# The last 256 tokens normalised as rows, a first layer with another order of transfers, splits and products, and low parts of fills on GpSimd: one change to a two-layer encoder step

## The chip, the cores and the metric

The kernel runs on one core of a Trainium2 chip. Its engines work side by side and meet at semaphores: the tensor engine (PE, with its weight loads PEld), VectorE (DVE), ScalarE (ACT), GpSimd (POOL), and SyncE (SP), which here issues all the transfers. The metric is the device time of one execution, in microseconds (us); lower is better.

## The reference

One step of a two-layer streaming encoder on 512 prompt tokens and 64 sample tokens (576 in all, `d_model` 1024). Everything is float32.

```
layer 0:  mixed = [ mLSTM(x), retention(x) ] from one input projection x @ w_in
          (4 heads each; per-head norm, gates; chunk by chunk), then mixed @ w_out
          x = LayerNorm(ALPHA * x + mixed @ w_out)
          x = LayerNorm(ALPHA * x + (silu(x @ w_g) * (x @ w_u)) @ w_down)
layer 1:  latent attention over past 256 rows and the new rows, with a chunk mask
          x = LayerNorm(ALPHA * x + attention(x) @ w_out)
          x = LayerNorm(ALPHA * x + (silu(x @ w_g) * (x @ w_u)) @ w_down)
```

The outputs are x of both groups and the states and cache rows that the layers leave.

## The kernel before

**Products in three parts.** Each float32 product is made of three products of a faster type: a value is split into a high part (ACT copies it into the type fp32r, L364 for weights, L600 for x) and a low part (the value less the high part, by a subtraction on DVE, L362 and L601). `fm` and `tm` issue high x high, low x high and high x low for each 128 rows of the contraction. `fm` gives a result with features on the partitions and tokens along the free dimension (weights stationary); `tm` gives rows, tokens on the partitions and 512 columns of features along it (activations stationary). `tms` is `tm` for the 64 sample tokens, with the high and low part of x side by side in the tile XS.

**Where activations lie.** Z holds x with features on the partitions, 8 blocks of 576 tokens. The tokens are handled in two halves, 0 to 319 and 320 to 575 in most stages (288 and 288 in some), and in five tiles: tile 0 is the 64 sample tokens, tiles 1 to 4 are 128 prompt tokens each; tiles 3 and 4 are half 1. Xh and Xl hold the parts of x, H those of hidden values.

**Weights.** `weight_pieces` lists the weights in the order of use; `Plan` packs them into blocks of 128 x 1024 (512 KB) and into fills of at most 512 columns. `dma_w` loads a block into one of three raw buffers (SP, L342), as soon as the program has issued both splits of an older block. `prefetch(i, lead)` splits fills in order, up to `lead` beyond the one in use, into a ring of 16 slots; a fill can be pinned to slots, and in layer 0 ten slots (`L0_SLOTS`) are in use, because the buffers of slots 8 to 13 hold other tiles. `self.hold` says below which fill a slot may be taken again.

**Order of the work.** The order on every engine is written out by the program: products are issued one after another, and tasks beside them (`spawn`, `tick`) are issued between products when a clock of issued product time passes their lags (`LAG`). `self.wait` issues waiting tasks with no product between. Nothing is reordered later: an instruction waits in its engine's queue, and so do all behind it.

**The start (`setup`, `layer0`).** x half 0 is loaded in pieces between the first weight blocks. For k = 0 to 7, tiles 1 and 2 of the retention's q and k (`rqrk`) are multiplied as their pieces come. At k = 3 the small tables (rope, ident, mask, cst, wg, bif) and at k = 3 and 4 the two pieces of x half 1 are issued on SP; x half 1 is split at k = 7, ahead of the evacuations `ev_qk` (L697 to L704, DVE) of tiles 1 and 2. Then follow the gates' product (`gate_mm`, L660 evacuates it), tiles 0, 3 and 4 of rqrk, the values `rv` and `mv` of all five tiles, and beside them the `gates` task and the five `retention` tasks. A retention task makes `s1` (scores into the single o bank and a bank of the mm group, masked by DVE, L928), `s2` (outputs, state update and head norm, ended by L970) and `s3` (transposes, evacuated to oT). The first mk product waits until all five `s3` are issued.

**The norms.** A LayerNorm of a half is fed by eight products (`ln_feed`: L1185 or L1187 adds the product to Z and so frees its bank; L1223, L1226 and L1233 keep sums and squares). `ln_finish` then makes the factors, and for each of the eight blocks subtracts the mean (L1265), scales (L1279), makes the high part and the biased value (ACT, L1311 and L1318), and the low part (POOL, L1319). Half 0 is scaled while PE still works at half 1.

**The end.** The last FFN ends with the down product in `fm` form for both halves (`down_units`, 8 blocks of 128 features, 7 rows of weights each), its norm in the same form, and stores of Z to `o_y`. For half 1 the norm and the stores come when PE has nothing more to do.

## Time and profile before

| | us |
|---|---|
| median of 3 runs (lowest, highest) | 1388.47 (1387.64, 1388.97) |
| profiled execution | 1387.13 |
| its span | 1385.4 |
| between the two | 1.73 |
| mean granted TensorE clock | 0.994 |

A line of the timeline gives the start, the time, the engine, the line of the kernel, the operation, the tiles (out<-in), the shape, the count, and in brackets how long the engine was idle before it and which instruction ended that. Several alike in a row are put together; the time then runs from the first start to the last end. Matmuls overlap in the pipeline, so that the pace is read from starts and not from durations. A wait for several things is put down to the one that seems to have come last. A group by form gives engine, operation, tiles, shapes, count | busy us, mean ns | idle us before, with the releasers.

### The profile page before, as it was taken

To read this page: it belongs to the slowest core of one execution; us is meant where nothing else is said; L and a number is where in the kernel's file an instruction comes from. 1 tells how busy PE (TensorE), PEld (TensorE's weight loads), DVE (VectorE), ACT (ScalarE), POOL (GpSimd) and SP (SyncE) were. 2 spreads that over 40 slices of the span, in tenths; PEclk is the share of its full clock that TensorE was granted. 3 is DMA by queue.
4 is the path that set the end of the run, shared out by engine and by line. 5 is a ranking of instruction groups with operands and counts; after the bars stand their busy time and mean duration, and the time that the engine had idled before them with its cause. 6 is when DMAs were issued, how large, how long until landed. Compare 5 with 4: busy or idle time off the path is not lost.

```text
span 1385.4 us, 24616 instructions
## 1 busy us (share of the span) xinstructions
PE 1348.3 (97%) x9759; PEld 1302.8 (94%) x9759; DVE 978.6 (71%) x2277; ACT 612.1 (44%) x1295; POOL 154.8 (11%) x182
## 2 busy tenths in 40 slices
PE   8999999999999999999999999999999999999995
PEld 6778999999999999999988899999999999999995
DVE  6666777678873685588898666667787358647877
ACT  4422333445551453255355466644555135425533
POOL 1100001115000000000021533311310000000000
PEclk9999999999999999999999999999999999999997
DMA  6111122511232123222322011130313312222221
GB/s 219 61 62 60 53 65 64 191 60 62 91 107 78 62 99 113 78 92 91 123 85 60 31 31 32 31 107 31 92 62 115 100 62 92 92 92 77 94 75 69
DMA packets 38235, 112.91 MB, mean 81 GB/s; under 512 B 5025, under 2 KB 12513, under 8 KB 38121
## 3 DMA queue, kind: packets, MB, share of 16 engines
q1 hardware_dynamic: 38120, 111.35, 24.4%
q8 instruction: 76, 1.25, 0.4%
q14 instruction: 39, 0.31, 0.1%
HBM read 107.45 MB, written 3.89 MB: 80 GB/s over the span
## 4 chain that ended last, share of the span: by engine, by line
PE 81%; DVE 12%; ACT 3%; DMA 2%; issue 2%; POOL 0%; SPq 0%; POOLq 0%; ACTq 0%; DVEq 0%
PE mm L465 42%; PE x L465 36%; DVE r L362 2%; PE x L533 2%; DVE Z L1279 1%; DMA raw<-in_w 1%; DVE Z L1265 1%; PE o L465 1%; ACT r L364 1%; ACT Xh L1311 1%; ACT Z L1318 0%; DMA Z<-in_x 0%; DVE small L543 0%; DVE small L542 0%; DVE small L541 0%
## 5 line engine op out<-in xcount | busy, mean ns | idle before, releaser
L465 PE MATMUL mm<-H,r 128*128 128x320 f32 (+2 forms) x2832 | 386.5, 296 | 0.0
L465 PEld LDWEIGHTS mm<-H,r 128*128 128x128 f32 x2832 | 377.2, 188 | 0.5 <-issue 0.2
L465 PE MATMUL x<-Xh,r 128*128 128x288 f32 x1216 | 244.7, 295 | 0.0
L465 PE MATMUL mm<-Xh,r 128*128 128x288 f32 (+2 forms) x1152 | 230.3, 298 | 6.0 <-DVE Z L1185 2.9
L364 ACT CAST r<-raw 128x512 fp32r<-128x512 f32 (+2 forms) x292 | 178.6, 648 | 104.9 <-PE mm L465 75.9
L362 DVE TENSOR_TENSOR r<-raw,r 128x512 fp32r<-128x512 f32 (+2 forms) x276 | 194.4, 734 | 37.7 <-ACT r L364 37.5
L465 PE MATMUL x<-r,r 128*128 128x288 f32 (+2 forms) x1534 | 211.7, 293 | 0.2 <-DVE r L1055 0.2
L465 PEld LDWEIGHTS x<-r,r 128*128 128x128 f32 x1534 | 205.9, 188 | 0.7 <-DVE r L1055 0.5
L465 PEld LDWEIGHTS x<-Xh,r 128*128 128x128 f32 x1216 | 194.5, 188 | 0.5
L465 PEld LDWEIGHTS mm<-Xh,r 128*128 128x128 f32 x1152 | 184.5, 190 | 7.2 <-ACT Z L1318 3.8
L465 PE MATMUL x<-Xl,r 128*128 128x288 f32 x608 | 179.2, 295 | 0.0
L465 PE MATMUL mm<-Xl,r 128*128 128x288 f32 (+2 forms) x576 | 167.5, 299 | 0.0
L364 ACT CAST r<-T 128x512 fp32r<-128x512 f32 (+1 forms) x114 | 87.1, 764 | 127.8 <-DVE T L397 109.1
L465 PEld LDWEIGHTS x<-Xl,r 128*128 128x128 f32 x608 | 114.0, 188 | 0.0
L362 DVE TENSOR_TENSOR r<-T,r 128x512 fp32r<-128x512 f32 (+1 forms) x114 | 96.3, 866 | 19.0 <-ACT r L364 19.0
L465 PEld LDWEIGHTS mm<-Xl,r 128*128 128x128 f32 x576 | 107.8, 190 | 0.1
L465 PE MATMUL mm<-r,Xh 128*128 128x512 f32 (+1 forms) x320 | 97.1, 385 | 4.4 <-DVE r L699 1.8
L1319 POOL TENSOR_TENSOR Xl<-Z,Xh 128x288 fp32r<-128x288 f32 (+2 forms) x36 | 30.9, 861 | 466.9 <-ACT Z L1318 466.4
L465 PEld LDWEIGHTS mm<-r,Xh 128*128 128x128 f32 x320 | 57.6, 188 | 17.3 <-issue 2.2
L1223 ACT ACTIVATE T<-Z 128x288 f32<-128x288 f32 (+2 forms) x56 | 24.9, 445 | 91.5 <-DVE Z L1185 47.1
L465 PE MATMUL mm<-r,Xl 128*128 128x512 f32 (+1 forms) x160 | 60.5, 378 | 0.0
L1580 DVE TENSOR_TENSOR T<-T,x 128x288 f32<-128x288 f32 x38 | 17.3, 454 | 58.7 <-PE x L465 58.7
(316 smaller groups left out, 1723.3 us busy)
## 6 DMA issues: line engine op xcount, KB each, us to landing
raw<-in_w SPq DMA_DIRECT2D x169, 512.0 KB, 3.5
r<-in_w SPq DMA_DIRECT2D x20, 512.0 KB, 3.5
Z<-in_x SPq DMA_DIRECT2D x1, 1280.0 KB
o_y<-Z SPq DMA_DIRECT2D x2, 640.0 KB, 3.3
Z<-in_x SPq DMA_DIRECT2D x2, 512.0 KB, 6.2
Z<-in_x SPq DMA_DIRECT2D x1, 1024.0 KB, 8.8
o_y<-Z SPq DMA_DIRECT2D x4, 256.0 KB, 2.1
Z<-in_x SPq DMA_DIRECT2D x3, 320.0 KB, 4.7
```

Of the source, the lines that this page charges most:

```text
L362: self.lo_engine.tensor_tensor(t[:, 1], src, t[:, 0].bitcast(F32), ALU.subtract)
L364: self.nc.scalar.copy(t[:, 0], src)
L465: self.nc.tensor.matmul(out, lhsT, rhs, start=start, stop=stop, skip_group_check=more)
L533: self.nc.tensor.transpose(out, in_, self.ident[0:n, 0:n])
L1223: nc.scalar.activation(q, z, AF.Square)
L1265: V.tensor_tensor(z, z, xd[:, 0:n], ALU.subtract)
L1279: V.scalar_tensor_tensor(z, z, gain(m), R[:, 0:n], ALU.mult, ALU.mult)
L1311: A.activation(self.Xh[:, a:b], z, AF.Identity, bias=bias(m))
L1319: G.tensor_tensor(self.Xl[:, a:b], z, self.Xh[:, a:b].bitcast(F32), ALU.subtract)
L1580: V.tensor_tensor(s[:, 0:n], s[:, 0:n], ps, ALU.add)
```

## The change

*Last 256 tokens as rows.* The down weights of the last seven rows of the last FFN are packed 512 features wide (`("dt", g)`), so that half 0 reads them in slices of 128 and half 1 as they are. After the eight units of half 0, each of the two 128-token tiles of half 1 is made in rows: identity products bring Z in, the down products add to it, `bn_stats` reads the banks, ACT subtracts the mean, DVE scales with the gain, and POOL (first tile) or DVE (second) adds the bias. The gain and the bias come as a broadcast row (`lnt`) into the buffer of Xh. The rows go to a new output `o_yt`.

*First layer.* Block 1 and its pieces of x are loaded in smaller parts; x half 1 is loaded to T1 ahead of the tables, at k = 1, and split in two parts behind the evacuations of tiles 1 and 2. The eight fills of rqrk, and later those of mv, lie in H (slots 16 to 23) and not in the ring; `cap` limits how far fills run ahead in each tile. `s1` of tile 1 uses an x bank, `s1` of tiles 2 to 4 follows the products of `s2` two tiles before; the head norm is `s2b`. The gates' last products come 4.5 later on the issue clock. The first mk product waits for the five `s2`.

*Norms.* While half 0 of a norm is scaled (`self.scaling`), a fill's low part is issued on POOL.

```diff
-L0_SLOTS = (0, 1, 2, 3, 4, 5, 6, 7, 14, 15)
+L0_SLOTS = (6, 7, 14, 15, 0, 1, 2, 3, 4, 5)
+FILLS_T = 8
...
+            if (li, f1) == (1, FT):
+                for g in range(2):
+                    for k in range(f0, f1):
+                        out.append(((("dt", g), k), "w_down", li, k * 128, [(512 * g, 512)]))
+                continue
...
+        self.cap = len(self.plan.fills)
+        for k in range(KT):
+            for nm in ("rqrk", "mv"):
+                self.pins[self.where[(nm, k)][0]] = (len(RING) + k,)
...
-            self.lo_engine.tensor_tensor(t[:, 1], src, t[:, 0].bitcast(F32), ALU.subtract)
+            (self.nc.gpsimd if self.scaling else self.lo_engine).tensor_tensor(t[:, 1], src, t[:, 0].bitcast(F32), ALU.subtract)
...
-            if j > min(i + (lead if j > last or len(self.plan.fills[j]) == 3 else qlead), last):
+            if j > min(i + (lead if j > last or len(self.plan.fills[j]) == 3 else qlead), last, max(i, self.cap)):
...
-            for k in (2 * j, 2 * j + 1) if j == 0 else (2 * j,):
-                e = k + 1 if j == 0 else k + 2
+            for k in (2 * j, 2 * j + 1) if j < 2 else (2 * j,):
+                e = k + 1 if j < 2 else k + 2
...
-                    self.dma_w(j, 2 if j == 0 else 1)
+                    self.dma_w(j, 2 if j < 2 else 1)
...
+                    self.cap = self.where[(name, KT - 1)][0] + ahead * (1 if len(tiles) == 1 else i + 1)
...
-            self.lead = 1 - k % 2 if k < KT - 1 else LEAD
+            self.lead = 1 - k % 2
             self.split_x(0, [k])
             if k == KT - 1:
                 self.split_wg()
-                self.split_x(1, range(KT))
...
-                if k == KT - 1:
-                    ev_qk(i, banks[i])
-            if k == 3:
+            if k == 1:
+                for j in range(2):
+                    nc.sync.dma_start(x1[:, 4 * j:4 * j + 4, :], half_dram(t["x"], 1, 4 * j, 4 * j + 4))
                 for name in ("rope", "ident", "mask", "cst"):
                     nc.sync.dma_start(getattr(self, name), t[name])
...
-            if k in (3, 4):
-                j = k - 3
-                nc.sync.dma_start(half_view(Z, 1, 4 * j, 4 * j + 4), half_dram(t["x"], 1, 4 * j, 4 * j + 4))
+        for i in (1, 2):
+            ev_qk(i, banks[i])
+            self.split_x(1, range(4 * i - 4, 4 * i), x1)
...
-        tm_units("rqrk", ev_qk, (0,))
-        tm_units("rqrk", ev_qk, (3,))
+        self.lead = 2 * KT
+        tm_units("rqrk", ev_qk, (0,), 2)
+        tm_units("rqrk", ev_qk, (3,), 5)
...
-        tm_units("rqrk", ev_qk, (4,))
-        tm_units("rv", ev_rv)
+        tm_units("rqrk", ev_qk, (4,), 8)
+        tm_units("rv", ev_rv, ahead=2)
...
-        tm_units("mv", ev_mv)
+        tm_units("mv", ev_mv, ahead=2)
+        self.cap, self.lead = len(self.plan.fills), LEAD
...
-                self.wait(lambda: self.ret_at["s3"] == NT)
+                self.wait(lambda: self.ret_at["s2"] == NT)
...
+        yield 4.5
+        x3 = self.xbank()
+        for h in range(4):
+            self.mm(x3[:, h * 8:h * 8 + 5], self.sel[:, h * 128:(h + 1) * 128], dec, True, True)
...
-            for o, bank in enumerate((self.obank(), self.bank())):
+            for o, bank in enumerate((self.xbank() if i == 1 else self.obank(), self.bank())):
...
-            s2(i)
+            O = s2(i)
+            if i + 2 < NT:
+                s1(i + 2)
+            s2b(i, O)
...
+        self.scaling = s.half == 0
...
-        self.chain(down_units(p, f0, f1), ahead)
+        if not last:
+            self.chain(down_units(p, f0, f1), ahead)
+            return
+        gb, rows = (self.st(x, [128, KT * NTOK]) for x in ("Xh", "Xl"))
+        nc.sync.dma_start(gb[:, 0:2048], self.t["lnt"].to_broadcast([128, 2048]))
+        gb = gb[:, 0:2048].rearrange("p (e f) -> p e f", e=2)
+        self.rel, self.lead = False, FILLS_T
+        for _, d in down_units(p, f0, f1):
+            d(0)
+            self.tick()
+        for i in range(2):
+            c = HN[0] + 128 * i
+...
+            banks = [self.bank(), self.obank() if i else self.bank()]
+            for g, ps in enumerate(banks):
+                for j in range(4):
+                    z = (4 * g + j) * NTOK + c
+                    self.mm(ps[:, 128 * j:128 * j + 128], Z[:, z:z + 128], self.ident, j == 0, False, more=True)
+                for k in range(f0, f1):
+                    wh, wl = self.wget((("dt", g), k))
+                    o = (k - f0) * NTOK + c
+                    xh, xl = H[:, o:o + 128], H[:, LO + o:LO + o + 128]
+                    self.mm(ps, xh, wh, False, False, more=True)
+                    self.mm(ps, xh, wl, False, False, more=True)
+                    self.mm(ps, xl, wh, False, k == f1 - 1, more=True)
+                    if k % 2:
+                        self.tick()
+                V.bn_stats(bs[:, g, :], ps)
+            V.bn_aggr(mv, bs)
+            V.tensor_scalar(nm, mv[:, 0:1], -1.0, None, ALU.mult)
+            y = [rows[:, (2 * i + g) * 512:(2 * i + g + 1) * 512] for g in range(2)]
+            for g, ps in enumerate(banks):
+                A.activation(y[g], ps, AF.Identity, bias=nm)
+            V.tensor_scalar(ve, mv[:, 1:2], LN_EPS, None, ALU.add)
+            self.rsqrt(rs, ve, None, tt)
+            for g in range(2):
+                V.scalar_tensor_tensor(y[g], y[g], rs, gb[:, 0, 512 * g:512 * g + 512], ALU.mult, ALU.mult)
+                (V if i else G).tensor_tensor(y[g], y[g], gb[:, 1, 512 * g:512 * g + 512], ALU.add)
+                nc.sync.dma_start(self.t["o_yt"][i, :, 512 * g:512 * g + 512], y[g])
```

## The prediction

> **What bounds the kernel now.** I read the head of the page first, then the timeline of the tensor engine (PE) for rows that carry a wait, and at each such row the timeline of the engine it names.

> ```profile
> span 1385.4 us, 24616 instructions
> PE 1348.3 (97%) x9759; PEld 1302.8 (94%) x9759; DVE 978.6 (71%) x2277; ACT 612.1 (44%) x1295; POOL 154.8 (11%) x182
> ```

> PE is busy for 97% of the span, so only two things can be gained: the 37.1 us in which it is idle, and PE work itself. The change alters almost no PE work. So the question is which idle stretches the edits reach. They lie in four places: the first products, the retention, the norms and the tail. I cost each place from its own rows.

> **1. First products.** These are rows of PE (the last number is the wait before the row, with its releaser), of ACT, and of VectorE (DVE).

> ```profile
> 9.67 0.50 PE L465 MATMUL mm<-r,Xh 128*128 128x512 f32 x1 [1.21 <-ACT r L364]
> ...
> 18.66 0.31 PE L465 MATMUL x<-Xh,wgp 128*16 128x320 f32 x1
> ...
> 26.75 0.70 PE L465 MATMUL mm<-r,Xh 128*128 128x512 f32 x2 [1.84 <-DVE r L699]
> ...
> 45.27 1.24 PE L533 MATMUL x<-ident,small 64*4 64x64 f32 x10
> ...
> 48.39 1.70 PE L465 MATMUL mm<-r,H 128*128 128x512 f32 x5 [1.18 <-DVE r L362]
> ```
> ```profile
> 11.16 1.14 ACT L364 CAST r<-raw 128x512 fp32r<-128x512 f32 x2 [0.30 <-DMA raw<-in_w]
> ...
> 13.27 1.14 ACT L364 CAST r<-raw 128x512 fp32r<-128x512 f32 x2 [0.25 <-DMA raw<-in_w]
> ...
> 16.80 0.25 ACT L594 CAST wgp<-T 128x64 fp32r<-128x64 f32 x1 [2.02 <-DMA T<-in_wg]
> ```
> ```profile
> 22.59 1.43 DVE L601 TENSOR_TENSOR Xl<-Z,Xh 128x256 fp32r<-128x256 f32 x4 [1.43 <-ACT Xh L600]
> 24.04 1.29 DVE L362 TENSOR_TENSOR r<-raw,r 128x512 fp32r<-128x512 f32 x2
> ...
> 39.85 0.16 DVE L829 TENSOR_TENSOR small<-x,bif 64x8 f32<-64x8 f32 x1 [1.96 <-issue]
> ...
> 42.96 0.18 DVE L849 TENSOR_TENSOR small<-small 128x20 f32<-128x20 f32 x1
> ```

> Before, the second half of x lands so late that DVE sits on its split until 24.0. The two qk evacuations behind it release their banks late, and PE waits 1.84. The weights of k=2 cost 1.21, and a late low part of rv costs 1.18.

> After, k=2 has its weights after fewer bytes (the block comes in two parts), which takes most of the 1.21 away. But the transfers are still the limit: between the rows at 11.16 and 13.27 lie a 320 KB and a 512 KB transfer, 832 KB in 2.11 us, or 394 KB per us. The blocks of k=4 to 7 land no earlier than now, so I count only 0.8 of the 1.21 at the end of k=7, where the gate product begins (18.66 before). Then the moved order takes something back. The two halves of x's second part (1024 KB) now stand on SP's queue ahead of rope, ident, mask, cst, wg and bif, where one weight block (512 KB) stood. That is 512 KB more, 1.3 us, so wg lands at 18.1 where it landed at 16.8. Its split (two steps of some 0.25) ends at 18.7. PE, which is free at about 17.9, waits for it with the gate product, and on DVE the two evacuations are queued behind it. The 0.8 is gone again.

> What is left is DVE's order. From 18.7 it has: the four evacuations and the gates' first part, which now take 25.3 to 43.1 less the 1.96 of waiting, 15.9; the split of x, 2 x 1.43 = 2.9; and the eight low parts of rv, which `ahead` 2, 5 and 8 lets in before the gates end, 8 x 0.65 = 5.2. 18.7 + 24.0 = 42.7. PE, without the 1.84, comes to the ten transposes that need the gates at 18.7 + (45.27 - 18.66 - 1.84) = 43.5, so the two meet: DVE is in time by under 1 us. They stood at 45.27; 1.8 is gained there and the 1.18 behind, since rv's low parts are then all made. I take **3.0**. The ends are 0 (rope and cst later than I think, and PE waiting for DVE) and 5.0 (all waits gone).

> **2. Retention.** Rows of PE.

> ```profile
> 78.54 0.37 PE L465 MATMUL o<-Z 64*128 64x128 f32 x1 [1.40 <-DVE r L928]
> ...
> 93.09 0.37 PE L465 MATMUL o<-Z 64*128 64x128 f32 x1 [1.27 <-DVE r L928]
> ...
> 120.44 0.60 PE L533 MATMUL mm<-ident,r 128*128 128x128 f32 x4
> ...
> 122.34 0.54 PE L465 MATMUL mm<-Xh,r 128*128 128x320 f32 x2
> ```

> `s1` writes into the single o bank and waits for the mask multiply of the tile before. With the x bank for tile 1, and with `s1(i + 2)` issued behind the products of `s2(i)`, the o bank was read long before: 2.67 gone. DVE's two mask steps move ahead of the head norm of the same tile, which then comes about 0.7 later and has a lag of 9 us before `s3` reads it. At the end PE does the last two sets of transposes and DVE's wait alone, from 120.44 to 122.34. Now the mk product may start after `s2`, and the two sets (0.60 each by the row) lie among its products: 1.90 - 1.20 = 0.7. The gates' `x3` products only move by some 4 us inside rv's products, which cover them. Sum 3.4; I take **3.0**, since DVE gets the mk fills here. Ends 0.5 and 4.2.

> **3. Norms.** Rows of PE, of DVE, of POOL, and POOL's group by form.

> ```profile
> 307.81 2.37 PE L465 MATMUL mm<-Xh,r 128*128 128x288 f32 x16 [2.66 <-ACT Z L1318]
> ...
> 971.05 0.51 PE L465 MATMUL mm<-Xh,r 128*128 128x288 f32 x2 [1.31 <-DVE Z L1185]
> 976.11 0.83 PE L465 MATMUL x<-cvec,T 128*128 128x2 f32 x6 [1.62 <-DVE T L1226]
> ```
> ```profile
> 302.15 1.49 DVE L362 TENSOR_TENSOR r<-raw,r 128x512 fp32r<-128x512 f32 x2 [2.44 <-ACT r L364]
> ...
> 307.22 0.45 DVE L1185 SCALAR_TENSOR_TENSOR Z<-Z,mm 128x288 f32<-128x288 f32 x1
> ...
> 307.95 1.07 DVE L1226 TENSOR_TENSOR T<-T,Z 128x288 f32<-128x288 f32 x1
> ...
> 962.48 1.49 DVE L362 TENSOR_TENSOR r<-raw,r 128x512 fp32r<-128x512 f32 x2 [1.84 <-ACT r L364]
> ```
> ```profile
> 307.78 1.92 POOL L1319 TENSOR_TENSOR Xl<-Z,Xh 128x288 fp32r<-128x288 f32 x2 [0.20 <-ACT Z L1318]
> ```
> ```profile
> L362 POOL TENSOR_TENSOR r<-raw,r 128x512 fp32r<-128x512 f32 x16 | 20.6, 1288 | 28.2 <-ACT r L364 28.2
> ```

> In the scaling of half 0 exactly two fills fall, in the first and in the third norm (the second has none, the fourth has no later fills). DVE waits 2.44 for ACT's cast and then works 1.49: 3.9 us in which the scaling stands still. Behind it L1185 at 307.22 frees the bank that PE waits 2.66 for (its end, 307.67, fits PE's 307.81 better than the ACT row named). With the two low parts on POOL, DVE is 3.9 us ahead and the bank is free. The new price is POOL's: 2 x 1.29 ahead of four Xl of half 0 (1.0 each, as at 307.78), from 302.1 on: the last Xl is made at 308.7. PE, from 305.15 with 16 products in 2.2 and seven more at 0.14, asks for it at 308.3: 2.66 - 0.4 = 2.2. In the third norm DVE is 3.3 ahead, and of 1.31 + 1.62 I take 1.6, because six more fills lie between the window and these waits. Sum **3.8**, ends 0.5 and 6.3.

> The row at 307.95 speaks against this edit: a step with both inputs in SBUF took 1.07 beside POOL's row of 307.78, where L1185, of the same size but with one input in PSUM, took 0.45. [...] By the rows it is 0.6 a step, on steps before only one of the three waits (976.11).

> **4. Tail.** Rows of PE, two of them from the start for a 512-wide product; then DVE's, SP's and the chain's end.

> ```profile
> 28.22 0.63 PE L465 MATMUL mm<-r,Xh 128*128 128x512 f32 x2
> ...
> 28.92 0.63 PE L465 MATMUL mm<-r,Xh 128*128 128x512 f32 x2
> ...
> 1320.14 9.40 PE L465 MATMUL mm<-H,r 128*128 128x320 f32 x63
> ...
> 1329.42 15.08 PE L465 MATMUL mm<-H,r 128*128 128x320 f32 x105
> ...
> 1352.51 0.72 PE L465 MATMUL x<-cvec,T 128*128 128x2 f32 x6
> ...
> 1354.30 5.21 PE L465 MATMUL mm<-H,r 128*128 128x256 f32 x42
> 1359.35 0.78 PE L465 MATMUL x<-T,ones 128*128 128x128 f32 x6
> 1359.93 7.70 PE L465 MATMUL mm<-H,r 128*128 128x256 f32 x63
> ```
> ```profile
> 1372.14 0.16 DVE L1255 SCALAR_TENSOR_TENSOR small<-small 128x2 f32<-128x2 f32 x1
> ...
> 1373.92 0.48 DVE L1261 TENSOR_SCALAR T<-ident,small 128x128 f32<-128x128 f32 x2
> ```
> ```profile
> 1321.18 3.70 SPq L342 DMA_DIRECT2D raw<-in_w  x2
> ```
> ```profile
> 1381.00 0.80 ACT Z L1298 x2
> ```

> Now PE ends at 1359.93 + 7.70 = 1367.6, and 17.8 us of norm and store follow. After: half 0 keeps its 168 products, 14.9 / 105 = 0.143 each, 24.0. Its norm keeps its small products, 1.8 (1352.51 to 1354.30) + 0.6 = 2.4. Half 1's 168 products of 256 columns become 2 x 2 x 7 x 3 = 84 of 512 columns at 0.233 (three in 0.70), 19.6. The 16 identity products that bring Z in as rows are fp32 of 128 columns: 0.58 us for 320 columns at 1359.35, so 0.23 each, 3.7. PE ends at 1320.1 + 49.7 + 0.2 = 1370.0, which is 2.4 later. Then come the statistics of the last group 0.7 (a 512-wide step as in part 1), four small steps 0.8, the square root's seven at 0.2 (nine small steps lie between 1372.14 and 1373.92) 1.4 with ACT's two centring passes beside them, and two scalings and two additions of 512 columns at 0.65, 2.6: 1375.5. From the last compute step (1381.8) to the end of the span now take 3.6 with the store: 1379.1. Gain **6.3**.

> The cover: half 0's norm (on DVE eight pairs of steps, each under the 0.65 of a 512-wide one, so under 10.4, and two stores) runs beside 23 us of row products, in steps at 16 ticks of which it needs some 13. The first product now needs seven fills where it needed two. Six of them are pinned to the same slots as now and done by 1321.2 (the sixth frees the block that the SP row starts to load), one every 0.65 against 0.43 of PE per fill, so 0 to 1 us. The `lnt` transfer (1024 KB) waits on SP for the last reader of Xh, at 1320; only the last weight block (issued at about 1324.5 in the row at 1321.18) stands behind it, and its fills are wanted some 98 products in, at 1334. Ends 3.5 and 8.0.

> **Sum.** 3.0 + 3.0 + 3.8 + 6.3 = 16.1. The profiled execution took 1387.13 (1.73 around the span), so 1371.0. The median of the three runs, 1388.47, is 1.34 above it: **1372.4**.

> **Rivals.** One row of a stage without waits (PE, PEld, DVE, ACT, POOL, then the granted clock) is needed for the last of them.

> ```profile
> 1200.00:1260.00 60.00, 60.00 (x456) 60.00 (x455) 28.36 (x49) 16.87 (x29) 0.00 (x0) 1.00 0.22 75
> ```

> [...] *(b) DVE stays the bound of the front*: rope and wg come last behind x, and the fills let in early stand ahead of the evacuations. For it: DVE has 24.0 us of work in 24. Parts 1 and 2 give 2.5 instead of 6.0: 1375.9. *(c) Half 0's norm is left over at the end*, and its steps stand ahead of the last rows on DVE: of the 10.4 half, 5, so the tail gives 1.3: 1377.4. Against it: 13 of 16 ticks. *(d) The change does nothing that can be seen*, every gain being given back by the wait behind it: 1388. *(e) Slower*: with the waits gone PE draws steadily, and its granted clock falls. From 1.2% on (1.2% of PE's 1348 us is 16.2) that eats all; at 2% it costs 27, and the time is 1399. Against it: PE was busy for all of those 60 us at a granted clock of 1.00.

> **Numbers.** Chances: forecast 0.53, a 0.15, b 0.15, c 0.10, d 0.04, e 0.03. If all four parts came out at their low ends they would give 4.5, at their high ends 23.5; they are apart from each other, so about half of each distance is likely: 1366.5 to 1378.5. a, b and c lie inside. With a little for waits that I have not seen the range is 1366 to 1380, which leaves out d, e and the far ends. A measurement of this kernel can tell about 0.2%, 2.8 us, from no change. Forecast, a, b and c are all faster by more: 0.93; d is 0.04 and e 0.03.

> **What would show it.** PE's rows: no wait at the second qk product of half 1, at most 1 us at the gate product, no wait for the mask multiply, the mk product right behind the last mv product. Two POOL rows of L362 in the first and two in the third norm, and PE's wait before the first gate under 0.7. PE's last product about 2.4 later in its stage than now (50 us after the stage starts) and 9 us from there to the end of the span. Wrong would be: a wait of several us at the first down product, POOL L362 followed by a PE wait of over 2 us, DVE steps of half 0's norm behind the last product, or a granted clock under 0.99 before the tail.

## The result, and the profile after

The changed kernel takes 1377.0 us in the median of four runs (1374.6 to 1378.6), the kernel before beside it 1388.7 (1387.6 to 1389.6): a ratio of 0.9916, with a 95% interval of 0.9904 to 0.9928. That is a gain of 11.7 us where 16.1 were forecast (1372.4); the time lies in the range given, 1366 to 1380. The profiled execution of the changed kernel took 1374.61, the shortest of its four.

The head of its page:

```profile
span 1372.8 us, 24434 instructions
...
PE 1347.9 (98%) x9692; PEld 1302.1 (95%) x9692; DVE 970.9 (71%) x2247; ACT 605.5 (44%) x1283; POOL 158.1 (12%) x184
```

PE works almost as long as before (1348.3); all but 0.4 of the 12.6 us by which the span is shorter are idle time. Line numbers have moved: products are now L483, the splits of weights L380 (low) and L382 (high), the low parts of a norm L1353. PE's timeline, with the places that the prediction spoke of:

```profile
18.23 0.32 PE L483 MATMUL x<-Xh,wgp 128*16 128x320 f32 x1 [0.32 <-DVE wgp L613]
...
41.30 1.48 PE L551 MATMUL x<-ident,small 64*4 64x64 f32 x10
...
69.02 2.00 PE L483 MATMUL mm<-H 128*128 128x512 f32 x8
...
112.01 0.54 PE L483 MATMUL mm<-Xh,r 128*128 128x320 f32 x2
...
298.79 0.40 PE L483 MATMUL mm<-Xl,r 128*128 128x288 f32 x1 [0.56 <-POOL Xl L1353]
...
319.98 0.53 PE L483 MATMUL mm<-Xh,r 128*128 128x288 f32 x2 [0.38 <-ACT Xh L1345]
321.32 0.53 PE L483 MATMUL mm<-Xh,r 128*128 128x288 f32 x2 [0.81 <-ACT Xh L1345]
...
1308.29 9.40 PE L483 MATMUL mm<-H,r 128*128 128x320 f32 x63
...
1321.27 0.43 PE L483 MATMUL x<-Z,ones 128*128 128x320 bf16 x1 [3.58 <-DVE Z L1220]
...
1358.96 5.15 PE L483 MATMUL o<-r,H 128*128 128x512 f32 x21
```

The prediction shows all the rows of before that these are read against but one, the first mv product:

```profile
74.46 2.03 PE L465 MATMUL mm<-r,H 128*128 128x512 f32 x8
```

Place by place: the ten transposes come at 41.30 instead of 45.27, the first mv product at 69.02 instead of 74.46 (5.4 gained), the first mk product at 112.01 instead of 122.34. The wait of 2.66 in norm 1 is 0.56. New is the wait of 3.58 us at 1321.27, in the stage that was to gain most. From the first of the last down products to the end of the span the stage took 1385.4 - 1320.14 = 65.3 us and now takes 1372.8 - 1308.29 = 64.5.

What stands behind the 3.58 is on DVE's timeline of the same kernel, and on SP's.

```profile
1311.39 2.56 DVE L380 TENSOR_TENSOR r<-raw,r 128x512 fp32r<-128x512 f32 x4
1315.78 1.29 DVE L380 TENSOR_TENSOR r<-raw,r 128x512 fp32r<-128x512 f32 x2 [1.83 <-ACT r L382]
1319.52 1.29 DVE L380 TENSOR_TENSOR r<-raw,r 128x512 fp32r<-128x512 f32 x2 [2.45 <-ACT r L382]
1320.73 1.28 DVE L1220 TENSOR_TENSOR Z<-Z,mm 128x320 f32<-128x320 f32 x3
```

```profile
1309.77 0.37 SPq L1710 DMA_DIRECT2D Xh<-in_lnt  x1
1312.71 0.33 SPq L359 DMA_DIRECT2D raw<-in_w  x1
```

PE had made three units by 1317.7, and the three evacuations (L1220) that free their banks stand on DVE behind the low parts of all fourteen fills of the stage. The last two of these wait for the last weight block, which is issued at 1312.71, behind the 1 MB of `lnt`, and splits only from 1318.9 on.

The second thing is on the view by windows: busy time of each engine in a stretch, then the granted clock, the share of the DMA engines and GB/s.

```profile
962.74:966.15 3.41, 2.02 (x17) 1.76 (x15) 3.41 (x8) 2.61 (x4) 0.00 (x0) 1.00 0.81 221
966.15:969.56 3.41, 3.41 (x16) 3.41 (x16) 2.94 (x16) 1.30 (x4) 0.00 (x0) 0.50 0.74 250
...
1317.72:1321.13 3.41, 0.00 (x0) 0.00 (x0) 1.61 (x3) 1.14 (x2) 0.00 (x0) 1.00 0.03 13
1321.13:1324.55 3.42, 3.28 (x13) 3.28 (x13) 3.39 (x10) 1.34 (x3) 0.00 (x0) 0.50 0.00 0
```

Behind the idle stretch the clock is 0.50 for 3.41 us: PE makes 13 products, where e3 (below) makes 25 in a stretch of the same length and the same stage at 1.00 (1321.30 to 1324.71). So the wait of 3.58 costs some 1.7 more. The first two rows show the same in the third norm; the kernel before has it there too (granted clock 0.80 and 0.77 in its stretches 976 to 980 and 980 to 984).

### The profile page after: what moved, and what is told of

It is laid out like the page before. It is cut to its first block, busy times and chain, and to the rows that moved or that the text cites. A ratio compares the mean times of both kernels' runs of the same rounds, so it can differ in the third digit from the quotient of the medians.

```text
span 1372.8 us, 24434 instructions
## 1 busy us (share of the span) xinstructions
PE 1347.9 (98%) x9692; PEld 1302.1 (95%) x9692; DVE 970.9 (71%) x2247; ACT 605.5 (44%) x1283; POOL 158.1 (12%) x184
## 4 chain that ended last, share of the span: by engine, by line
PE 80%; DVE 9%; issue 5%; ACT 2%; DMA 2%; POOL 1%; SPq 0%; POOLq 0%; DVEq 0%; ACTq 0%
PE mm L483 41%; PE x L483 36%; PE x L551 2%; DVE r L380 2%; PE o L483 1%; DVE Z L1313 1%; DMA raw<-in_w 1%; ACT r L382 1%; DVE Z L1298 1%; POOL Xl L1353 0%; DMA Z<-in_x 0%; DMA T<-in_wg 0%; ACT Xh L1345 0%; DVE small L559 0%; DVE small L560 0%
## 5 line engine op out<-in xcount | busy, mean ns | idle before, releaser
L483 PE MATMUL mm<-H,r 128*128 128x256 f32 (+2 forms) x2664 | 367.6, 298 | 0.0
L483 PEld LDWEIGHTS mm<-H,r 128*128 128x128 f32 x2664 | 358.6, 189 | 4.1 <-issue 3.6
L483 PE MATMUL x<-Xh,r 128*128 128x288 f32 x1216 | 244.7, 295 | 0.1
L483 PE MATMUL mm<-Xh,r 128*128 128x288 f32 (+2 forms) x1152 | 230.7, 298 | 3.4 <-DVE Z L1218 2.1
L382 ACT CAST r<-raw 128x512 fp32r<-128x512 f32 (+2 forms) x276 | 168.8, 648 | 99.1 <-PE mm L483 73.2
L483 PE MATMUL x<-r,r 128*128 128x288 f32 (+2 forms) x1534 | 211.7, 293 | 0.2 <-DVE r L1088 0.2
L483 PEld LDWEIGHTS x<-r,r 128*128 128x128 f32 x1534 | 205.9, 188 | 0.6 <-DVE r L1088 0.5
L380 DVE TENSOR_TENSOR r<-raw,r 128x512 fp32r<-128x512 f32 (+2 forms) x256 | 182.8, 742 | 22.0 <-ACT r L382 21.9
L483 PEld LDWEIGHTS x<-Xh,r 128*128 128x128 f32 x1216 | 194.5, 188 | 0.8 <-DVE T L1630 0.3
L483 PEld LDWEIGHTS mm<-Xh,r 128*128 128x128 f32 x1152 | 184.5, 190 | 4.6 <-ACT Xh L1345 2.0
L483 PE MATMUL x<-Xl,r 128*128 128x288 f32 x608 | 179.2, 295 | 0.0
L483 PE MATMUL mm<-Xl,r 128*128 128x288 f32 (+2 forms) x576 | 167.8, 299 | 0.6 <-POOL Xl L1353 0.6
L382 ACT CAST r<-T 128x512 fp32r<-128x512 f32 (+1 forms) x114 | 86.9, 762 | 127.2 <-DVE T L415 114.8
L483 PEld LDWEIGHTS x<-Xl,r 128*128 128x128 f32 x608 | 114.0, 188 | 0.0
L380 DVE TENSOR_TENSOR r<-T,r 128x512 fp32r<-128x512 f32 (+1 forms) x114 | 96.3, 865 | 18.6 <-ACT r L382 18.6
L483 PEld LDWEIGHTS mm<-Xl,r 128*128 128x128 f32 x576 | 107.8, 190 | 0.9 <-POOL Xl L1353 0.8
L1353 POOL TENSOR_TENSOR Xl<-Z,Xh 128x288 fp32r<-128x288 f32 (+2 forms) x36 | 30.6, 855 | 462.9 <-ACT Z L1352 462.5
L483 PE MATMUL mm<-r,H 128*128 128x512 f32 (+3 forms) x323 | 60.3, 339 | 0.1
L1256 ACT ACTIVATE T<-Z 128x288 f32<-128x288 f32 (+2 forms) x49 | 21.8, 447 | 84.2 <-DVE Z L1218 49.4
L483 PE MATMUL mm<-r,Xh 128*128 128x512 f32 (+1 forms) x192 | 55.2, 371 | 0.9 <-ACT Z L1352 0.9
L1645 DVE SCALAR_TENSOR_TENSOR Z<-Z,mm 128x320 f32<-128x320 f32 (+1 forms) x32 | 14.3, 453 | 59.1 <-PE mm L483 59.1
```

Source lines behind the costliest of these rows:

```text
L380: (self.nc.gpsimd if self.scaling else self.lo_engine).tensor_tensor(t[:, 1], src, t[:, 0].bitcast(F32), ALU.subtract)
L382: self.nc.scalar.copy(t[:, 0], src)
L483: self.nc.tensor.matmul(out, lhsT, rhs, start=start, stop=stop, skip_group_check=more)
L1256: nc.scalar.activation(q, z, AF.Square)
L1353: G.tensor_tensor(self.Xl[:, a:b], z, self.Xh[:, a:b].bitcast(F32), ALU.subtract)
L1645: V.scalar_tensor_tensor(z, z, ALPHA, ps[:, 0:HN[half]], ALU.mult, ALU.add)
```

## The experiments

Every ratio is to the kernel before, run on the same chip. One stretch of 3.41 us at half clock (0.50) is 1.7 us, and how many there are differs from run to run; so small differences are read from one place of the profile as well, and not from the medians alone.

| | median us | ratio (95%) |
|---|---|---|
| changed kernel | 1377.0 | 0.9916 (0.9904 to 0.9928) |
| e1, splits 5 ahead | 1372.5 | 0.9883 (0.9869 to 0.9896) |
| e2, rows' transfer later | 1373.1 | 0.9882 (0.9866 to 0.9898) |
| e3, both | 1369.3 | 0.9868 (0.9853 to 0.9883) |
| e4, tail as before | 1378.2 | 0.9921 (0.9909 to 0.9934) |
| e5, low parts on DVE | 1378.9 | 0.9926 (0.9914 to 0.9939) |
| e6, retention as before | 1380.0 | 0.9943 (0.9930 to 0.9955) |
| e7, x split first | 1376.6 | 0.9910 (0.9895 to 0.9925) |
| e8, rqrk and mv in the ring | 1375.0 | 0.9903 (0.9889 to 0.9916) |
| e9, transfers as before | 1376.7 | 0.9914 (0.9896 to 0.9932) |
| e10, e7 and e9 | 1376.9 | 0.9923 (0.9898 to 0.9947) |
| e11, front as before | 1381.4 | 0.9948 (0.9933 to 0.9964) |
| e12, e3 with a filled wait | 1369.0 | 0.9863 (0.9847 to 0.9879) |

**Where the tail's gain went: e1, e2, e3, e4.** First the order of the splits alone.

```diff
-FILLS_T = 8
+FILLS_T = 5
```

> The splits may run 5 fills ahead of the products in the last down product instead of 8, nothing else. With 8, the trace of the changed kernel shows all fourteen splits of the stage in front of the first evacuation on VectorE, the last two at 1319.52 us, and TensorE idle for 3.58 us at 1321.27 us; behind it the granted clock is 0.50 and 0.74 for some 4 us. Theory 1, the order of the splits costs the gain: with 5, the last block's two splits come behind the fourth unit, the idle 3.58 us go, the clock stays at 1.00 (1.6 us), and the run is 4 to 5 us shorter, 1370 us profiled and 1372 in the median. Theory 2, the transfer of the gain and bias rows ahead of the last weight block costs it: that block still lands at about 1318.8 us, its products wait for it instead, and the time stays within 1 us of the changed kernel's 1377.0.

PE's timeline of e1:

```profile
1310.43 9.40 PE L483 MATMUL mm<-H,r 128*128 128x320 f32 x63
1319.68 0.32 PE L483 MATMUL x<-Z,ones 128*128 128x320 bf16 x1
...
1326.33 0.41 PE L483 MATMUL mm<-H,r 128*128 128x320 f32 x1 [1.06 <-ACT r L382]
1327.06 10.41 PE L483 MATMUL mm<-H,r 128*128 128x320 f32 x68 [0.32 <-DVE r L380]
```

The product at 1319.68 follows the 63 without a wait, and no stretch of this stage is at half clock while PE works. 4.5 us gained in the median, as theory 1 had it. The wait of 1.06, 99 products into the stage and so in the fifth unit (the expectation of e3 says the sixth), is the price of splitting too late; it is not the transfer, since ACT's cast at 1325.68 waited for none, and ACT had been idle for 2.71 us just before.

Then the transfer alone. In the program `lnt` is issued behind the eight units; SP runs ahead of the others (in e12, where the transfers have this order too, it issues `lnt` at 1311.85, and PE is at the eight units until 1331.8), so what this changes is that the rows stand behind the last weight block on SP's queue and not ahead of it.

```diff
-        nc.sync.dma_start(gb[:, 0:2048], self.t["lnt"].to_broadcast([128, 2048]))
...
         for _, d in down_units(p, f0, f1):
             d(0)
             self.tick()
+        nc.sync.dma_start(gb.rearrange("p e f -> p (e f)"), self.t["lnt"].to_broadcast([128, 2048]))
```

> The 1 MB transfer of the gain and bias rows is issued behind half 0's eight units instead of ahead of them; the splits still run 8 fills ahead. Theory 1 (order of the splits): the splits still stand in front of the first evacuation, but the last block lands some 2.5 to 3 us earlier (1 MB at the 380 GB/s of that stretch takes 2.7 us), so that 3.58 us of idle shrink to 0.5 to 1.5 us, the clock does not fall behind so short a wait, and the run is 3 to 4.5 us shorter, median 1372.5 to 1374. Theory 2 (the transfer): the wait goes altogether, 4 to 5 us, median 1372. Theory 3, the clock falls for a reason of its own at this place: the granted clock of 0.50 to 0.74 is there although the wait is short, and only 2 to 3 us are gained, median 1374.5.

PE's timeline of e2:

```profile
1322.38 0.30 PE L483 MATMUL x<-Z,ones 128*128 128x320 bf16 x1 [1.26 <-DVE Z L1220]
```

1.26 instead of 3.58, no fall of the clock behind it, 3.9 us gained in the median: what theory 1 gave, not theory 2, since the splits still stand in front. The last block's split on ACT begins 8.3 us into the stage (1319.99, the stage starting at 1311.72) where it began 10.6 into it (1318.87). So each of the two cures takes most of the loss, because the loss needs both: all splits in front of the evacuations, and the last block late. Both cures together, with the lead back at 8 from the third unit on:

```diff
-        for _, d in down_units(p, f0, f1):
+        for m, (_, d) in enumerate(down_units(p, f0, f1)):
+            self.lead = FILLS_T if m < 2 else 8
```

> Both cures of the last stage together: the gain and bias rows are transferred behind half 0's units, and the splits run 5 fills ahead in the first two units and 8 from the third on. Alone, the shorter lead left 1.06 and 0.32 us of wait in the sixth unit, and the later transfer 1.26 us at the first evacuation. Theory: the last block lands at about 1315.8 us, its two splits stand behind the second evacuation, no wait of over 0.5 us is left in the stage, and the run is 1 to 1.5 us shorter than with either cure alone: 1371.3 to 1372 us in the median, 5 to 6 below the changed kernel. Rival: the two waits have one cause, ScalarE's and VectorE's queues, and only change place: 1372.5 to 1373.

PE's and DVE's timelines of e3:

```profile
1308.78 9.40 PE L483 MATMUL mm<-H,r 128*128 128x320 f32 x63
1318.02 0.32 PE L483 MATMUL x<-Z,ones 128*128 128x320 bf16 x1
...
1354.27 5.15 PE L483 MATMUL o<-r,H 128*128 128x512 f32 x21
```

```profile
1313.59 2.53 DVE L380 TENSOR_TENSOR r<-raw,r 128x512 fp32r<-128x512 f32 x4 [0.42 <-ACT r L382]
1316.04 0.88 DVE L1220 TENSOR_TENSOR Z<-Z,mm 128x320 f32<-128x320 f32 x2
1317.35 1.29 DVE L380 TENSOR_TENSOR r<-raw,r 128x512 fp32r<-128x512 f32 x2 [0.43 <-ACT r L382]
```

Two evacuations now stand in front of the last pair of splits, and the stage has no wait left. It takes 1368.1 - 1308.78 = 59.3 us, 5.9 less than before the change, where the forecast had 6.3. The median is 7.7 below the changed kernel, more than was expected by 2, where the profiled executions differ by 4.7 (1374.61 and 1369.91) and the stage by 5.2; what the medians have beyond that no place in the profiles shows. The four runs lie between 1368.3 and 1373.7, at mean clocks of 0.998 to 0.995.

With the last stage as before (the fills, the units, the norm and the stores of the kernel before; the rest changed):

> The change without its last part: the last down product and its norm are the kernel before's, the first layer and the scaling windows stay changed. From the two traces the last stage is 0.75 us shorter in the changed kernel (64.5 against 65.26 us). Theory: this kernel is 0.5 to 1.5 us slower than the changed one, 1377.5 to 1378.5 us in the median, and without its swings of 4 us from run to run, since the wait with the low clock behind it is what swings. Rival: the last part is worth the 6.3 us that were forecast and the stages ahead are worth less than the traces say: 1383 us.

PE's timeline of e4 has the two waits of before again (2.14 and 2.83 there):

```profile
1358.29 0.61 PE L474 MATMUL x<-cvec,T 128*128 128x2 f32 x4 [2.14 <-DVE T L1250]
...
1362.77 1.22 PE L474 MATMUL x<-T,ones 128*128 128x128 f32 x4 [2.63 <-DVE T L1285]
```

The median is 1.2 us above the changed kernel's, but the intervals of the two ratios overlap, so the medians alone don't tell them apart. The stage does: it takes 1374.0 - 1308.66 = 65.3 us, as before the change, against 64.5. So the rows were worth some 0.8 us as they stood. Half of the expectation failed: this kernel swings from run to run as much as the other (1375.8 to 1379.4), so the stall is not what swings alone.

**The norms: e5.**

```diff
-            (self.nc.gpsimd if self.scaling else self.lo_engine).tensor_tensor(t[:, 1], src, t[:, 0].bitcast(F32), ALU.subtract)
+            self.lo_engine.tensor_tensor(t[:, 1], src, t[:, 0].bitcast(F32), ALU.subtract)
```

> The changed kernel with all low parts on VectorE, those of the scaling windows too. From the two traces the stretch of norm 1 became 0.6 to 0.8 us shorter and that of norm 3 1.2 us. Theory: 1.9 us slower than the changed kernel, 1378.9 us in the median, with a wait of 2 to 3 us on VectorE's low part in norm 1. Rival, the forecast's sum: 3.8 us slower, 1380.8. Rival, the edit is worth nothing: within 0.5 us of 1377.0.

PE's timeline of e5, then POOL's and DVE's of the changed kernel in the same norm:

```profile
297.98 3.66 PE L483 MATMUL mm<-Xh,r 128*128 128x288 f32 x16 [2.64 <-ACT Z L1352]
```

```profile
292.45 2.80 POOL L380 TENSOR_TENSOR r<-raw,r 128x512 fp32r<-128x512 f32 x2
295.21 3.52 POOL L1353 TENSOR_TENSOR Xl<-Z,Xh 128x288 fp32r<-128x288 f32 x4
```

```profile
286.59 0.45 DVE L1259 TENSOR_TENSOR T<-T,Z 128x288 f32<-128x288 f32 x1
...
294.02 1.55 DVE L1259 TENSOR_TENSOR T<-T,Z 128x288 f32<-128x288 f32 x1
```

The wait of before is back, and the median is 1.9 us higher, what the two traces gave, though the two intervals overlap. Right behind this wait e5's profile has the clock at 0.50 for 3.41 us; the kernel before has the same wait without it. The edit does what was said in norm 1: POOL's two low parts end at 295.2, the last Xl at 298.7, and PE asks for it 0.56 us too soon. But DVE's step with two inputs in SBUF, which takes 0.45 while POOL has nothing to do (286.59), took 1.55 beside POOL's second low part.

**The first layer: e6 to e11.** The retention's part alone undone:

```diff
-            if i < 2:
-                while at["s1"] < i or self.qk_done < NT:
-                    yield
+            while at["s1"] < i or at["s2"] < i - 1 or self.qk_done < NT:
+                yield
...
-                self.wait(lambda: self.ret_at["s2"] == NT)
+                self.wait(lambda: self.ret_at["s3"] == NT)
```

> The changed kernel with the retention as before: s1 of a tile is its own step, tile 1 uses the o bank, and the mk product waits for s3. Between the start of the first mv product and that of the first mk product TensorE now needs 43.0 us where it needed 47.9. Theory of the traces: 2.7 us of that are the waits for the o bank, 0.3 and 1.9 us the end of the retention in front of mk, so that 4 to 5 us come back: 1381 to 1382 us. The forecast's sum: 3.0 us, 1380.0. Rival, the weights that now lie in H let the products run on and only they give it: under 1.5 us, below 1378.5.

PE's timeline of e6:

```profile
69.86 2.00 PE L483 MATMUL mm<-H 128*128 128x512 f32 x8
...
72.94 0.37 PE L483 MATMUL o<-Z 64*128 64x128 f32 x1 [0.43 <-DVE r L953]
...
87.40 0.37 PE L483 MATMUL o<-Z 64*128 64x128 f32 x1 [1.28 <-DVE r L953]
...
116.70 1.28 PE L551 MATMUL mm<-ident,r 128*128 128x128 f32 x4 [1.67 <-DVE r L995]
...
117.74 0.54 PE L483 MATMUL mm<-Xh,r 128*128 128x320 f32 x2
```

The waits for the o bank and the one in front of mk are back, the first of them smaller (0.43, where it was 1.40). From the first mv product to the first mk product e6 needs 117.74 - 69.86 = 47.9 us, as the kernel before did, and the changed kernel 43.0: this edit alone makes the 4.9 of this stretch. The median is only 3.0 higher, the forecast's sum, but it holds what the clock did elsewhere: this profile has no half clock in the third norm, where the changed kernel's has 1.7 us of it. What the run also settles is that the weights in H are not what gives this part: they are still there.

Then the front in pieces. e7 splits x's second half ahead of the evacuations again, e8 takes the pins into H away, e9 puts the transfers back, e10 is e7 and e9 together, e11 undoes all of the front (slots, caps and leads too).

```diff
 e7          if k == KT - 1:
                 self.split_wg()
+                self.split_x(1, range(KT), x1)
 e9 -            if k == 1:
+            if k == 3:
...
+            if k in (3, 4):
+                j = k - 3
+                nc.sync.dma_start(x1[:, 4 * j:4 * j + 4, :], half_dram(t["x"], 1, 4 * j, 4 * j + 4))
```

> The changed kernel with the split of x's second half ahead of the two qk evacuations again, and all of it at k = 7; the transfers stay in the new order. Theory, VectorE's order: TensorE waits again for a bank of the two evacuations behind the gate products, 1.5 to 3 us, since the eight steps of the split take 2.9 us on VectorE, and the run is 1.5 to 3 us slower than the changed kernel: 1378.5 to 1380. Rival, the forecast's own row of VectorE work: the order only moves work about in front of the gates, which are the bound, and the time stays within 0.7 us of 1377.0.

> The changed kernel with the split weights of rqrk and mv in the ring's ten slots as before, instead of in slots of their own in H; the order, the caps and the leads stay. Theory: with ten slots the fills of rv can't be made ahead while rqrk is read, so the wait at the first rv product returns (1.2 us before), and the products of rqrk and mv run at 0.70 us for three instead of 0.68 (some 70 threes, 1.2 us): 1.2 to 3 us slower, 1378.2 to 1380. Rival, only the order of the steps counts: within 0.7 us of 1377.0.

> The changed kernel with the first transfers as before: the second weight block whole, rope, ident, mask, cst, wg and bif ahead of x's second half, and that half at k = 3 and 4; the order of the splits stays the new one. The old split order alone (with the new transfers) moved the first mv product by only 0.2 us, to 69.58. Theory A, late data and old order are both needed for the 1.84 us of before: with the two evacuations ahead of the split, late data costs nothing, and the first mv product starts at 69.4 plus 0 to 0.8 us (for the weights of k = 2). Theory B, the transfers alone carry the gain: the first mv product starts at 71 to 72 us.

> The same with the old order of the splits as well (x's second half split ahead of the two evacuations). Theory A: now both causes are there, TensorE waits some 1.8 us for a bank behind the gate products, and the first mv product starts at 71 to 72.5 us. Theory B: as with the old transfers alone. Rival: the caps and leads of the fills carry the front, and the first mv product still starts at 69 to 70 us.

> The changed kernel with the whole first layer ahead of the retention as before: transfers, splits, slots, caps and leads; the retention, the norms and the tail stay changed. Theory of the traces: the first mv product starts at 74.3 us instead of 69.0 to 69.7, about 5 us later, and the whole is 5 us slower than the changed kernel, 1382 us in the median, give or take the 1.7 us of a window at half clock. The forecast's sum: 3.0 us, 1380.

The start of the first mv product is what to compare; the changed kernel, e1 to e6 and e12, which share the changed front, have it between 68.9 and 69.9. One row of PE's timeline for each of e7, e8 and e9, then three of e10 and two of e11:

```profile
69.58 2.00 PE L483 MATMUL mm<-H 128*128 128x512 f32 x8
```

```profile
70.05 2.02 PE L480 MATMUL mm<-r,H 128*128 128x512 f32 x8
```

```profile
69.49 2.00 PE L483 MATMUL mm<-H 128*128 128x512 f32 x8
```

```profile
25.26 0.70 PE L483 MATMUL mm<-H,Xh 128*128 128x512 f32 x2 [0.66 <-DVE r L720]
...
29.55 0.33 PE L551 MATMUL x<-ident,r 128*128 128x128 f32 x1 [0.87 <-DVE r L723]
...
71.60 2.00 PE L483 MATMUL mm<-H 128*128 128x512 f32 x8
```

```profile
27.11 0.70 PE L476 MATMUL mm<-r,Xh 128*128 128x512 f32 x2 [1.90 <-DVE r L710]
...
74.83 2.03 PE L476 MATMUL mm<-r,H 128*128 128x512 f32 x8
```

Late data alone costs nothing (69.49), the old order alone costs nothing (69.58, so that e7's theory failed and its rival held), both together 2 us (71.60): theory A. The two edits secure the same gain twice. All of the front is worth 5 to 6 us (74.83), so some 3 of them lie in what e10 leaves in place: slots, caps and leads. Of these the slots in H alone are at most 0.5 or so (70.05 is hardly outside the spread of the shared front); the caps and leads were not undone by themselves. e8's expectation was too high, and its median, 2.0 below the changed kernel, is no gain that a place in the profile shows. In e9 to e11 the medians follow with 1376.7, 1376.9 and 1381.4; e10's is 2 too low for its place, within what stretches at half clock make of it.

**The clock: e12.** To e3 are added nine products whose result is overwritten by the next product into that bank.

```diff
+        if s.which == 2 and s.half:
+            for _ in range(9):
+                nc.tensor.matmul(xd[:, 0:n], self.Xh[:, 0:128], self.Xh[:, 0:n], start=True, stop=True, skip_group_check=True)
```

> The kernel with both cures of the last stage, and nine products of 288 columns (0.133 us each, 1.2 us) whose result is thrown away, in front of the first small products of half 1's third norm, where TensorE waits 1.41 us for VectorE. In ten of eleven profiles of changed kernels the granted clock fell to 0.50 for 3.41 or 6.83 us right behind that place, 1.7 us of loss for each 3.41. Theory, the clock is granted by TensorE's activity in stretches of 3.41 us: the wait is full of work, no stretch there is under 0.75 busy, the clock stays at 1.00 at that place, and the run is 1.5 to 2 us shorter than with the two cures alone (1369.3 us in the median, 1369.8 profiled): 1367.3 to 1367.8, with a ratio to the kernel before of 0.985. Rival, the clock falls for what follows (the small products, or the change to the next product): the fall stays, and the time is the same within 0.5 us, or longer by up to 0.3 us.

PE's timeline of e12, then the stretch by windows in e12 and in e3:

```profile
962.88 1.34 PE L1283 MATMUL x<-Xh 128*128 128x288 f32 x9
964.52 0.80 PE L483 MATMUL x<-cvec,T 128*128 128x2 f32 x6 [0.30 <-DVE T L1259]
```

```profile
964.37:967.78 3.41, 3.26 (x25) 3.18 (x26) 3.22 (x10) 3.21 (x6) 0.00 (x0) 1.00 0.77 252
```

```profile
963.49:966.90 3.41, 2.15 (x16) 2.05 (x17) 3.38 (x9) 2.88 (x5) 0.00 (x0) 1.00 0.74 240
966.90:970.31 3.41, 3.41 (x16) 3.41 (x15) 2.98 (x16) 1.03 (x3) 0.00 (x0) 0.50 0.67 216
```

The clock stayed at 1.00, and the profiled execution took 1368.2 where e3's took 1369.9: 1.7 less, as the theory had it (the fall had been there in eleven of twelve profiles, the kernel of e6 being the twelfth). The medians, 1369.0 and 1369.3, don't tell the two kernels apart, and one profile is one draw: e6's had no fall there either, with nothing filled in. So that the filled wait holds the clock is likely, and not shown; that TensorE's activity grants it stays the theory of the expectation. e12 and e3 are the shortest kernels of the study.

## Why the prediction was right in sign and 4.6 us off

| part | forecast | in the profiled execution |
|---|---|---|
| front (to the first mv product) | 3.0 | 74.46 - 69.02 = 5.4 |
| retention (mv to mk) | 3.0 | 47.9 - 43.0 = 4.9, of which 0.4 comes back behind mk: 4.5 |
| norms | 3.8 | 11.85 ahead of the last down product, 9.92 ahead of norm 1 (the product x<-Z at 201.11 that is now at 191.19): 1.9 |
| tail | 6.3 | 65.3 - 64.5 = 0.8 |
| sum | 16.1 | 12.6 |

*The step that failed* is the tail's cover: "only the last weight block stands behind it, and its fills are wanted some 98 products in, at 1334". Wanted at 1334, they were issued at the start. With a lead of 8, the seven fills of the first unit bring the other seven with them, in the program's order, on ACT and DVE, ahead of the first evacuation. e1 and e2 show the two conditions of the wait, and e3 that it goes with both. I asked when PE needs the fills, and not what is queued behind the splits that wait for them. The prediction had listed "a wait of several us at the first down product" as a sign of being wrong; it came three units later, at 1321.27. Its price is the 3.58 and the 1.7 of half clock behind it. The rest of the tail's working holds: e3 has PE's end at 1359.4, 50.6 after the stage starts (forecast 50), and 8.7 from there to the end (forecast 9). Rival c gave 1377.4, nearly the measured time, by a mechanism that didn't happen: half 0's norm was done on DVE before the statistics of the last rows (1361.5 and 1364.1).

*Front, too small.* The step was "so the two meet: DVE is in time by under 1 us", with PE at 43.5 and DVE at 42.7. They met, but both earlier: PE came at 41.30, and DVE made its last step for the gates at 41.36, beside the first of the ten. The stretch from the gate product to the transposes took 26.61 us before (18.66 to 45.27) and takes 23.07 (18.23 to 41.30), so 3.5 went and not 1.84: beside it a wait of 0.41 at 30.63 of before (e11 has it again at 30.99), and smaller pieces that I have not added up, among them threes of 512 columns that take 0.68 with weights in H (24.23 to 24.91) where they took 0.70. The sum of all waits was given as the upper end, 5.0; that is about what came. The reason given, DVE's order, was half of it: e7 and e9 show that the order or the transfers alone would do.

*Retention, right in kind.* 2.67 and the end in front of mk (1.90, now 0.36 for one set, with 0.4 paid later) make 3.8 of the 4.5; the forecast had computed 3.4 and then took 0.4 off for a conflict with mk's fills that the trace doesn't show.

*Norms, half.* In norm 1 the arithmetic was right (2.66 - 0.56 = 2.1, forecast 2.2), and 0.7 went again at 320 us, where half 1's norm on ACT became the late one (0.38 + 0.81 against 0.48); some 0.5 more I have not located. Norm 3 gave 1.2 of 1.6. The prediction's 0.6 for a DVE step with two SBUF inputs beside POOL was too small for one step and too large for the other: of the two beside POOL's two low parts, one took 1.55 (294.02), 1.1 more than alone (286.59), and the other 0.45 (293.65); norm 3 has the same pair, 1.55 at 952.50 and 0.45 at 952.13. The part came out at 1.9, half of its forecast. No run shows the low value that chance a stands for; what the runs show in its place is these rows.

*The sum and the range.* Front and retention gave 3.9 more than was forecast, norms and tail 7.4 less; that the time still lies in the range is in part luck, since the errors of the four parts made up for half of each other. The range has a slip of its own: half of the distance to the high ends is (23.5 - 16.1) / 2 = 3.7, which gives 1368.7 as the lower bound, and not 1366.5.

*Granted clock.* Rival e expected it to fall under steady load. In the changed kernel it stayed at 1.00 from 969.57 to 1317.72, with PE busy for 348.1 of the 348.2 us, and fell to 0.50 behind waits instead (from 966.15 and from 1321.13); its mean is 0.996, before 0.994.

## What to carry to other kernels

When the order on each engine is fixed by the program, a prefetch is not free because its data are wanted late: ask which evacuation stands behind the split that waits for the transfer. Price an idle stretch of TensorE with what the clock does behind it (here some 1.7 us behind one of 3.58). If two edits each remove one of two conditions of a wait, undoing either shows nothing; only undoing both shows what they are worth.

## What the runs showed of the hardware

So at 962.74 a stretch with 1.4 us of waiting was enough. But the time that PE is busy doesn't decide it alone. Here is such a stretch of e1, with no fall behind it:

```profile
1323.69:1327.10 3.41, 2.03 (x13) 1.55 (x12) 3.17 (x8) 1.50 (x3) 0.00 (x0) 1.00 0.00 0
```

The kernel before had PE busy for 1.57 of the 3.41 us from 305.97, in which 1.84 of its wait of 2.66 lie, and the clock stayed at 1.00. In e5 it fell behind a stretch with 2.63 (from 967.61). At 320 us, behind the same waits of 0.38 and 0.81, the clock fell in the profiles of e2, e7, e8 and e9 and not in those of the changed kernel, e1 and e3: in e9 behind a stretch with 2.15 us of work, and in e3 not behind one with 2.14. What a stretch must hold isn't settled. That the number of falls differs from run to run I take for what spreads the changed kernel's runs over 4 us: their mean clocks are 0.993 to 0.996, and 0.003 of 1375 us is 4.1.
